# Softmax weights transposed by TensorE for every fourth query tile, in a fused attention and Fourier layer with a hand-written order on all engines

## The chip, the cores and the metric

One core of a Trainium2 chip runs the whole layer in one launch. The metric is the device time of one execution in microseconds. The numbers below come from three timed runs and from one further execution under the hardware profiler.

## What is computed

One trunk layer over 1024 latent tokens and 256 context tokens, model width 1024, all in float32. After a modulated layer norm and one input projection, one half of the mixing width is attention with 8 heads (96 query and key dimensions, 64 value dimensions, 1280 keys), the other half a 2-D Fourier mix. Both are gated, concatenated, projected and normalised. The part that matters here:

```python
def _softmax_attend(q, k, v):
    s = jnp.einsum("bqhd,bkhd->bhqk", q, k).astype(jnp.float32) * (1.0 / math.sqrt(QK_DIM))
    p = jax.nn.softmax(s, axis=-1).astype(v.dtype)
    return jnp.einsum("bhqk,bkhv->bqhv", p, v)
...
y = jnp.concatenate([attn * jax.nn.silu(g_mla), four * jax.nn.silu(g_f)], axis=-1)
return y @ w_out + b_out          # then x_new = layer_norm(alpha * x + gate * y) * g + b
```

## The kernel before

To keep float32 accuracy, operands are split into a high and a low part, and a product is three matmuls (high by high, high by low, low by high). The engines are called PE (TensorE, matmuls), DVE (VectorE), ACT (ScalarE), POOL (GpSimd) and SP (SyncE, which issues the DMAs).

The projections and the Fourier part run first (up to 277 us). Then a loop of 34 iterations handles 32 pairs of query tiles: a pair is one head and two tiles (j = 0, 1) of 128 queries. For a tile the steps are:

- `s_lat` (PE): scores against 1280 keys in three blocks a, b (512 columns each) and c (256), into the PSUM tile `SS[j]`;
- `max_lat` (DVE): one pass out of `SS[j]` that copies the negated scores to `E` in SBUF and keeps their minimum, a bias for the exponent; `bias` adds a constant to it;
- `exp` (ACT): the exponential in place in `E`, with the row sum;
- `hi` (ACT): the float16 high part `EH[:, 0]`; `lo` (POOL): the low part `EH[:, 1] = E - EH[:, 0]`, and then a transposing DMA, issued by SP, of both parts into `ET`, which has the keys on the partitions;
- `pv` (PE), two iterations later (`LAG = 2`), for both tiles of the pair: V by `ET` into a PSUM tile of the pool `tr`; `pv_top` (ACT) and `pv_out` (DVE) add its two halves into the attention output.

PSUM has 8 banks: `SS[0]` and `SS[1]` have three each (1280 of 1536 columns used), the pool `tr` has two buffers of one bank. `tr` also serves the fill work: keys (`build_kt`), V of the second half of the heads (`build_v`), queries (`build_qt`) and row factors (`finish_pair`), which are transposed or multiplied on PE and split by ACT and DVE. In SBUF, `E` and `EH` have three buffers of one tile, `ET` three of one pair.

Iteration n does the scores of pair n+1 (`nxt`), the late steps of pair n (marked with ') and the PV product of pair n-2. The string `SEQ` (`SEQ2` from n = 30) names the steps in order: S scores, m minimum, t bias, x exponential, h and l the two parts, P0 and P1 the halves of PV, Ra and Rv `pv_top` and `pv_out`, f one piece of fill work, `ga` and `gv` its postponed ACT and DVE parts, s one step of weight preparation, E output matmuls. The order is binding for PE alone (`MAN = 'P'`); on the other engines a planner with a cost model orders the instructions, and it may put later output matmuls into the loop.

Weight preparation (`prep(kt)`, kt = 0 to 7) makes the operands of the output projection: it loads 128 rows of `w_out`, multiplies them by a gate (DVE), splits them (POOL the high part, DVE the low part) and splits the mixed activations the same way. Row blocks 4 and 5 are prepared from iterations 24 and 27 in halves, 6, 7, 0 and 1 from iterations 30 to 33 in one piece, 2 and 3 behind the loop. The tail multiplies 8 token tiles by 8 row blocks (`out_mms`), adds, normalises (`finish`) and stores.

Of the kernel before, what the change touches and what calls it, by code (L numbers as in the profile page):

```python
# [21 lines left out]
P = 128  # L22
# [4 lines left out]
QK = 96  # L27
# [6 lines left out]
MAN = 'P'  # L34
SEQ = "ga S0 h1' l1' f P0 P1 ga Ra Rv m0 t0 s x0 s h0 l0 S1b S1c E0 E3 gv S1a m1 t1 f gv E2 x1 E1".split()
# [6 lines left out]
BIA = 'v'  # L42
SEQ2 = "S0c S0a h1' E1 l1' P0 S0b S1c P1 ga Ra Rv m0 t0 x0 h0 s s l0 ga S1b E0 E3 f gv S1a m1 t1 f gv E2 x1".split() or SEQ
# [19 lines left out]
def tile_hybrid_block(ctx: ExitStack, tc: tile.TileContext, a, out, dbg=None):  # L63
# [919 lines left out]
    pools["tr"] = at_ctx.enter_context(tc.tile_pool(name="ps_tr2", bufs=2, space=PSUM, reuse_waits="tile"))  # L983
    ps_s = at_ctx.enter_context(tc.tile_pool(name="ps_s", bufs=1, space=PSUM, reuse_waits="tile"))

    SS = [ps_s.tile([P, 1536], F32, tag=f"SS{j}", name=f"SS{j}") for j in range(2)]

    class Pair:
        def __init__(self, n):
            self.n, self.h, self.pr = n, n // 4, n % 4  # L990
            self.grp, self.e = self.h // 4, self.h % 2
            self.E, self.EH, self.ET = [None, None], [None, None], None
            self.mx = None
            self.po = None

# [132 lines left out]
    def prep(kt, alloc=None, n=1, parts=None):  # L1128

        raw = alloc(f"wor{kt}") if alloc else u4([P, D], F32, f"wor{kt}")  # L1130
        nc.sync.dma_start(out=raw, in_=a["w_out"][kt * P:(kt + 1) * P, :])
        part = parts or (lambda name: u4([P, D], F32R, name))
        wo[kt] = (part(f"woh{kt}"), part(f"wol{kt}"))
        mix[kt] = (part(f"mh{kt}"), part(f"ml{kt}"))
# [56 lines left out]
    early = {(0, 0): (0, 0), (0, 1): (0, 1), (1, 0): (1, 0), (1, 1): (1, 1)}  # L1191
    done = {}
# [6 lines left out]
    with tc.manual_schedule(engines={ET.PE}):  # L1199
        VA, VB = eval('(1,3)')  # L1200
        for i2 in range(VA):
            build_v(0, i2, False)
        p0.s_lat(0, 0)
        p0.s_lat(0, 1)
        p0.s_lat(0, 2)
        for i2 in range(VA, VB):
            build_v(0, i2, False)
        p0.max_lat(0)
        p0.bias(0)
        p0.exp(0)  # L1210
        if "h0'" not in SEQ:
            p0.hi(0)
        if "l0'" not in SEQ:
# [18 lines left out]
    with tc.manual_schedule(engines={{'P': ET.PE, 'V': ET.DVE, 'A': ET.Activation, 'G': ET.Pool, 'S': ET.SP}[c] for c in MAN}):  # L1232
        for n in range(NP + LAG):
# [4 lines left out]
            if n % 4 == 3 and n < NP - 1:  # L1238
                sum_rows(n // 4)
            fill = fills[n]  # L1240
            if n in FT['s']:
                steps += prep(4 + FT['s'].index(n), n=2)
            if n in LATE:
                steps += prep(ORDER[2 + LATE.index(n)])
            for op in (SEQ2 if n >= NSEQ2 else SEQ):
# [6 lines left out]
                if c in "SCmtxhlPR" and who is None:  # L1252
                    continue
# [4 lines left out]
                elif c == "m":  # L1258
                    who.max_lat(k)
                elif c == "t":  # L1260
# [59 lines left out]
    for kt in ORDER[2 + len(LATE):]:  # L1320
        for step in prep(kt, tl, parts=tw if kt in ORDER[-2:] else None):
# [50 lines left out]
    for t in range(3, 7):  # L1372
        ps = po_t(t)
        for i in range(8):
# [4 lines left out]
                  (tr("o70"), SS[1][:, 1024:1280], SS[0][:, 0:256])))  # L1379
# [75 lines left out]
```

## Time and profile before

| | us |
|---|---|
| three timed runs: median, lowest, highest | 634.28, 633.05, 636.16 |
| profiled execution: time, span of its instructions | 637.83, 636.1 |
| busy in the span: PE, DVE, ACT, POOL | 587.2, 391.9, 296.6, 302.1 |
| mean granted TensorE clock, share of full speed | 0.963 |

The span runs from the first to the last instruction of the profiled execution. An engine's busy time counts what it executes; waiting, branching and the issue of DMAs are not in it. Matmuls overlap each other, so that a matmul's own duration is longer than the distance to the next one, and PE's busy share is higher than its use. The granted clock is 1 at 2.4 GHz and 0.5 at 1.2 GHz. Times in the rows below count from the span's start.

### The profile page before, as it was taken

Reading aid. Unit: us, or ns where it says so; the run is one execution under the profiler, and the core shown is the slowest. Engines: PE = TensorE matmul, PEld = TensorE weight load, DVE = VectorE, ACT = ScalarE, POOL = GpSimd, SP = SyncE. Lnnn points to the kernel's source line nnn. Section 1 sums busy time; section 2 is a strip of 40 time slices with the busy share of each in tenths; the row PEclk is TensorE's granted clock in tenths of the full one; section 3 lists DMA queues with packets and bytes.
Section 4 is the critical chain, followed back from the end, with each engine's and each line's share of the span. In section 5 each row is a group of like instructions: output and inputs, shape, how many; then the busy total and the mean of one; then the engine's idle time right before and its main releaser. Section 6 shows DMA issues by size and latency. Waiting matters only on the chain.

```text
span 636.1 us, 9339 instructions
## 1 busy us (share of the span) xinstructions
PE 587.2 (92%) x3491; PEld 472.2 (74%) x3491; DVE 391.9 (62%) x742; ACT 296.6 (47%) x464; POOL 302.1 (47%) x233
## 2 busy tenths in 40 slices
PE   7999999999999998999999878999889877989994
PEld 6887777888899998988666656776656655668884
DVE  5538218611016588777566663677476887899567
ACT  2423521310125345488888895789678652100000
POOL 2123216011014186458768865787679876850000
PEclk8999999999999999999989987999889889899998
DMA  9999028000001122108999998799999998722302
GB/s 283 316 316 366 6 82 287 13 1 0 1 0 51 61 76 101 30 13 168 189 164 191 180 186 156 130 170 177 205 166 196 213 197 166 290 72 93 141 33 99
DMA packets 199701, 88.80 MB, mean 140 GB/s; under 512 B 168204, under 2 KB 189964, under 8 KB 199656
## 3 DMA queue, kind: packets, MB, share of 16 engines
q1 hardware_dynamic: 199656, 88.21, 59.7%
q8 instruction: 27, 0.44, 0.3%
q14 instruction: 18, 0.15, 0.1%
HBM read 41.39 MB, written 4.20 MB: 72 GB/s over the span
## 4 chain that ended last, share of the span: by engine, by line
PE 53%; DVE 14%; ACT 11%; DMA 8%; issue 6%; POOL 6%; SPq 1%; DVEq 0%; POOLq 0%; ACTq 0%
PE g L320 11%; PE fin L320 8%; PE SS L1154 7%; DMA ET<-EH 5%; ACT E L1029 4%; ACT EH L1038 4%; POOL EH L1046 4%; PE o L1154 3%; DVE E L1016 3%; DVE ml L83 2%; PE pv L1063 2%; PE tm L135 2%; PE tm L136 2%; PE tm L137 2%; PE SS L135 2%
## 5 line engine op out<-in xcount | busy, mean ns | idle before, releaser
L1046 POOL TENSOR_TENSOR EH<-E,EH 128x1280 f16<-128x1280 f32 x64 | 169.3, 2650 | 51.1 <-ACT EH L1038 41.8
L1016 DVE TENSOR_SCALAR_CACHE_REDUCE E<-SS 128x1280 f32<-128x1280 f32 x64 | 95.3, 1488 | 39.0 <-PE SS L137 27.0
L1029 ACT ACTIVATE E<-E,mx 128x1280 f32<-128x1280 f32 x64 | 86.8, 1357 | 23.9 <-DVE mx L1023 23.4
L1038 ACT ACTIVATE EH<-E 128x1280 f16<-128x1280 f32 x64 | 81.1, 1267 | 13.4 <-DMA ET<-EH 12.4
L1063 PE MATMUL pv<-ET,V 128*128 128x256 f16 x320 | 52.2, 300 | 18.8 <-DMA ET<-EH 6.5
L320 PE MATMUL fin<-h,wh 128*128 128x512 f32 x192 | 65.2, 407 | 0.0
L320 PE MATMUL g<-h,wh 128*128 128x512 f32 x192 | 60.2, 394 | 1.0 <-DVE upm L382 1.0
L135 PE MATMUL SS<-KTh,QT 96*128 96x512 f32 x128 | 56.3, 440 | 4.2 <-DVE E L1016 3.6
L1063 PEld LDWEIGHTS <-V 128*128 128x128 f16 x320 | 28.8, 105 | 35.9 <-issue 19.5
L136 PE MATMUL SS<-KTl,QT 96*128 96x512 f32 x128 | 51.8, 405 | 0.0
L137 PE MATMUL SS<-KTh,QT 96*128 96x512 f32 x128 | 51.8, 405 | 0.0
L320 PEld LDWEIGHTS fin<-h,wh 128*128 128x128 f32 x192 | 36.2, 189 | 10.3 <-issue 2.9
L320 PEld LDWEIGHTS g<-h,wh 128*128 128x128 f32 x192 | 36.0, 188 | 9.8 <-issue 1.4
L351 POOL TENSOR_SCALAR h<-xnT,mod 128x512 f32<-128x512 f32 x15 | 12.9, 859 | 63.2 <-ACT xnT L337 27.6
L111 ACT ACTIVATE rs_t<-mvf,eps 128x1 f32<-128x1 f32 x8 | 2.2, 293 | 81.4 <-DVE mvf L1342 77.3
L320 PE MATMUL g<-h,wl 128*128 128x512 f32 x96 | 37.8, 394 | 0.0
L320 PE MATMUL fin<-h,wl 128*128 128x512 f32 x96 | 37.1, 395 | 0.0
L1066 PE MATMUL pv<-ET,V 128*64 128x256 f16 x320 | 36.3, 304 | 0.0
L135 PEld LDWEIGHTS SS<-KTh,QT 96*128 96x128 f32 x128 | 24.9, 194 | 14.0 <-issue 6.6
L429 ACT ACTIVATE gt<-g,cols 128x512 f32<-128x512 f32 x12 | 8.1, 689 | 56.1 <-PE g L320 56.1
L1154 PE MATMUL SS<-woh,mh 128*128 128x512 f32 (+1 forms) x96 | 31.3, 384 | 2.4 <-POOL mh L82 1.3
L1352 POOL TENSOR_TENSOR xr<-xr,lng 128x256 f32<-128x256 f32 x2 | 1.4, 726 | 65.0 <-ACT xr L1351 65.0
(330 smaller groups left out, 1402.8 us busy)
## 6 DMA issues: line engine op xcount, KB each, us to landing
wada<-in_w_ada_dram SPq DMA_DIRECT2D x32, 256.0 KB, 6.0
x<-in_x_dram SPq DMA_DIRECT2D x8, 512.0 KB
wgate<-in_w_ada_dram SPq DMA_DIRECT2D x8, 512.0 KB, 6.6
wor<-in_w_out_dram SPq DMA_DIRECT2D x8, 512.0 KB, 4.1
xr<-in_x_dram SPq DMA_DIRECT2D x8, 512.0 KB, 9.9
out_dram<-xr SPq DMA_DIRECT2D x15, 256.0 KB, 2.1
wr<-in_w_in_dram SPq DMA_DIRECT2D x6, 512.0 KB, 5.5
wtr<-in_w_in_dram SPq DMA_DIRECT2D x4, 416.0 KB, 6.7
```

The source lines that it names most:

```text
L135: nc.tensor.matmul(ps, lhsT=sh, rhs=mh, start=(start and i == 0), stop=False)
L136: nc.tensor.matmul(ps, lhsT=sh, rhs=ml, start=False, stop=False)
L137: nc.tensor.matmul(ps, lhsT=sl, rhs=mh, start=False, stop=(i == n - 1))
L320: nc.tensor.matmul(ps, lhsT=(w.hi, w.lo, w.hi)[p][k][:, cs], rhs=h[:, p // 2], start=(k == 0 and p == 0), stop=(k == 7 and p == 2))
L351: nc.gpsimd.tensor_scalar(out=h, in0=xt, scalar1=sc, scalar2=sh, op0=ALU.mult, op1=ALU.add)
L1016: nc.vector.tensor_scalar(out=self.E[j], in0=SS[j][:, 0:1280], scalar1=0.0, scalar2=3e38, op0=ALU.add, op1=ALU.min, accum_out=self.mx[:, 2 ...
L1029: nc.scalar.activation(out=self.E[j], in_=self.E[j], func=AF.Exp, scale=-1.0, bias=self.mx[:, j:j + 1], accum_out=sums[self.h][:, qt:qt + 1])
L1038: nc.scalar.activation(out=o, in_=i, func=AF.Copy)
L1046: {"v": nc.vector, "p": nc.gpsimd}[eng].tensor_tensor(out=self.EH[j][:, 1, cs], in0=self.E[j][:, cs], in1=self.EH[j][:, 0, cs], op=ALU.sub ...
L1063: nc.tensor.matmul(po, lhsT=v.rearrange("p l c -> p (l c)"), rhs=e, start=(kt == 0), stop=False)
L1066: nc.tensor.matmul(po[64 * g:64 * g + 64], lhsT=v[:, 0], rhs=e, start=False, stop=(kt >= 8), tile_position=(0, 64 * g))
L1154: nc.tensor.matmul(ps[c], lhsT=st, rhs=w[:, c[0]:c[1]], start=(i == 0 and st is mh and w is wh), stop=(i == 7 and st is ml))
```

## The change

The scores of a pair go to three PSUM tiles: `SL[0]` and `SL[1]` (1024 columns, two banks each) for blocks a and b, and one shared bank `SC` for block c of both tiles. The freed bank gives `tr` a third buffer. The minimum is taken in two passes (`max_lat` over 1024, a new step c, `max_ctx`, over 256 columns), which the bias step joins.

For tile 1 of every pair with even n (16 of 64 tiles), `hi`, `lo` and the transposing DMA are replaced: PE transposes `E` in ten 128x128 blocks, in three groups of 4, 4 and 2 blocks, each in a `tr` buffer (T, `e_tr`); ACT copies the group to the high part in `ET` and DVE subtracts it for the low part (U, `e_out`). All five engines' orders are now the written one (`MAN = 'PVAGS'`), with new strings. Weight preparation starts at iterations 20, 23, 26 and 29 for blocks 4 to 7 and at 31 and 32 for 0 and 1, in halves, with the loads of `w_out` up to two iterations earlier; from iteration 30 on and in the tail ACT takes the high parts in place of POOL. Eight groups of output matmuls are named in the order. The diff, cut to its core:

```diff
-MAN = 'P'
-SEQ = "ga S0 h1' l1' f P0 P1 ga Ra Rv m0 t0 s x0 s h0 l0 S1b S1c E0 E3 gv S1a m1 t1 f gv E2 x1 E1".split()
+MAN = 'PVAGS'
+ON_PE = {(n, 1) for n in range(0, 32, 2)}
+KCUT = ((0, 1, 2, 3), (4, 5, 6, 7), (8, 9))
+SEQ = "S0b x1' gv S0a P0 s m0 P1 S0c l0' f c0 Ra h1' t0 Rv l1' gv T1a' S1b S1a U1a' T1b' m1 S1c T1c' ga x0 c1 ga t1 s U1b' h0 f U1c'".split()
-SEQ2 = "S0c S0a h1' E1 l1' P0 S0b S1c P1 ga Ra Rv m0 t0 x0 h0 s s l0 ga S1b E0 E3 f gv S1a m1 t1 f gv E2 x1".split() or SEQ
+SEQ2 = "S0b x1' gv S0a E P0 s s m0 P1 E E S0c l0' f c0 Ra h1' t0 Rv l1' gv T1a' S1b S1a U1a' T1b' m1 S1c T1c' ga x0 c1 ga t1 s s U1b' h0 f U1c' s s".split()
-LATE = eval('(30, 31, 32, 33)')
+INSIDE = (((4, 18, 20), (5, 22, 23), (6, 26, 26), (7, 28, 29)), ((0, 30, 31), (1, 31, 32)))
-FT = eval("{'k': [0, 0, 1], 'q': [1, 2], 'r': 4, 'p': [5, 5], 'v': [14, 14, 15, 15, 15], 'g': 22, 's': [24, 27]}")
+FT = eval("{'k': [0, 0, 1], 'q': [1, 2], 'r': 4, 'p': [5, 5], 'v': [11, 14, 15, 16, 17], 'g': 18}")
...
-    pools["tr"] = at_ctx.enter_context(tc.tile_pool(name="ps_tr2", bufs=2, space=PSUM, reuse_waits="tile"))
+    pools["tr"] = at_ctx.enter_context(tc.tile_pool(name="ps_tr2", bufs=3, space=PSUM, reuse_waits="tile"))
...
-    SS = [ps_s.tile([P, 1536], F32, tag=f"SS{j}", name=f"SS{j}") for j in range(2)]
+    SL = [ps_s.tile([P, 1024], F32, tag=f"SL{j}", name=f"SL{j}") for j in range(2)]
+    SC = ps_s.tile([P, 512], F32, tag="SC", name="SC")
...
+        def minimum(self, j, src, dst, c):
+            nc.vector.tensor_scalar(out=dst, in0=src, scalar1=0.0, scalar2=3e38, op0=ALU.add, op1=ALU.min,
+                                    accum_out=self.mx[:, c:c + 1])
...
+            self.minimum(j, SL[j], self.E[j][:, 0:1024], 2 + j)
+        def max_ctx(self, j):
+            self.minimum(j, SC[:, 256 * j:256 * j + 256], self.E[j][:, 1024:1280], 4 + j)
         def bias(self, j):
+            nc.vector.tensor_scalar(out=self.mx[:, j:j + 1], in0=self.mx[:, 2 + j:3 + j], scalar1=self.mx[:, 4 + j:5 + j],
+                                    scalar2=LIFT, op0=ALU.min, op1=ALU.add)
...
+        def e_tr(self, j, c):
+            self.weights_t()
+            kts = KCUT[c]
+            pt = self.pt[j, c] = tr("et")
+            for i, kt in enumerate(kts):
+                nc.tensor.transpose(pt[:, i * P:(i + 1) * P], self.E[j][:, kt * P:(kt + 1) * P], ident)
+        def e_out(self, j, c, what="av"):
+            k0, n = KCUT[c][0], len(KCUT[c])
+            pt = self.pt[j, c][:, 0:n * P].rearrange("p (k q) -> p k q", q=P)
+            hi, lo = self.ET[:, j, k0:k0 + n], self.ET[:, j, 10 + k0:10 + k0 + n]
+            if "a" in what:
+                nc.scalar.activation(out=hi, in_=pt, func=AF.Copy)
+            if "v" in what:
+                nc.vector.tensor_tensor(out=lo, in0=pt, in1=hi, op=ALU.subtract)
...
+    def load_wo(kt, alloc=None):
+        raws[kt] = alloc(f"wor{kt}") if alloc else u4([P, D], F32, f"wor{kt}")
+        nc.sync.dma_start(out=raws[kt], in_=a["w_out"][kt * P:(kt + 1) * P, :])
...
-        return {c: SS[c[0] // 512][:, 1024:1536] for c in HALVES}
+        return {HALVES[0]: SC, HALVES[1]: tr(f"o{t}")}
...
-    early = {(0, 0): (0, 0), (0, 1): (0, 1), (1, 0): (1, 0), (1, 1): (1, 1)}
+    early = [(t, i) for i in range(len(INSIDE[0])) for t in range(2)]
...
-            if n in FT['s']:
-                steps += prep(4 + FT['s'].index(n), n=2)
-            if n in LATE:
-                steps += prep(ORDER[2 + LATE.index(n)])
+            for kt, r, _ in INSIDE[0] + INSIDE[1]:
+                if n == r:
+                    load_wo(kt)
+            for kt, _, r in INSIDE[0] + INSIDE[1]:
+                if n == r:
+                    steps += prep(kt, how=split_ps if n >= NP - 2 else None)
...
-    for kt in ORDER[2 + len(LATE):]:
-        for step in prep(kt, tl, parts=tw if kt in ORDER[-2:] else None):
+    for kt in ORDER[sum(map(len, INSIDE)):]:
+        load_wo(kt, tl)
+        for step in prep(kt, 1, tw, split_ps):
```

## Rows read from the trace of the kernel before

**Rows 1.** Windows, by stage: busy us (instructions) of each engine, granted clock, DMA share, GB/s.

```profile
0.00:277.00 277.00, 269.07 (x1677) 232.51 (x1678) 136.74 (x311) 90.39 (x185) 81.51 (x118) 0.99 0.37 115
...
296.70:435.30 138.60, 126.51 (x786) 93.22 (x784) 85.10 (x162) 115.27 (x154) 103.46 (x50) 0.94 0.96 172
435.30:522.10 86.80, 74.88 (x447) 53.09 (x447) 62.52 (x102) 63.70 (x84) 68.52 (x38) 0.92 1.03 191
...
544.10:636.10 92.00, 80.52 (x369) 65.06 (x368) 75.37 (x127) 4.71 (x12) 20.42 (x12) 0.96 0.32 115
```

**Rows 2.** Timeline of PE: the start of the last pair's PV product.

```profile
540.70 0.71 PE L1063 MATMUL pv<-ET,V 128*128 128x256 f16 x5 [3.10 <-DMA ET<-EH]
```

**Rows 3.** Timeline of PE, one pair early in the loop: start us, us, what.

```profile
302.64 0.70 PE L1063 MATMUL pv<-ET,V 128*128 128x256 f16 x5
...
304.81 0.50 PE L135 MATMUL SS<-KTh,QT 96*128 96x512 f32 x1
...
305.38 0.39 PE L137 MATMUL SS<-KTh,QT 96*128 96x512 f32 x1
305.61 0.28 PE L135 MATMUL SS<-KTc,QT 96*128 96x256 f32 x1
```

**Rows 4.** Waits of PE in the loop, us in total, times, longest.

```profile
PE SS L135 <- DVE E L1016: 7.1, 3, 3.5
PE pv L1063 <- DMA ET<-EH: 6.5, 6, 3.1
PE pv L1063 <- DVE KTl L774: 5.9, 3, 3.2
PE pv L1063 <- DVE mx L1023: 3.9, 3, 1.8
```

**Rows 5.** Windows, same columns: the stretch in the loop that holds two long waits.

```profile
377.50:391.20 13.70, 11.12 (x47) 7.68 (x48) 7.25 (x15) 10.27 (x15) 7.86 (x3) 0.62 0.98 187
```

**Rows 6.** Lines by form in the loop: count | busy us, mean ns | idle before, releaser.

```profile
L1016 DVE TENSOR_SCALAR_CACHE_REDUCE E<-SS 128x1280 f32<-128x1280 f32 x62 | 92.3, 1488 | 38.2 <-PE SS L137 26.1 <-POOL EH L1046 9.4 <-PE pv L1066 1.6
...
L774 DVE TENSOR_TENSOR V<-v,V 128x512 f16<-128x512 f32 x7 | 4.7, 680 | 1.4 <-ACT V L772 1.3
...
L774 DVE TENSOR_TENSOR KTc<-kt,KTc 64x256 fp32r<-64x256 f32 x4 | 1.7, 421 | 0.4 <-ACT ckc_k L772 0.2 <-ACT KTc L772 0.2
...
L1029 ACT ACTIVATE E<-E,mx 128x1280 f32<-128x1280 f32 x63 | 85.5, 1357 | 23.7 <-DVE mx L1023 23.2
L1038 ACT ACTIVATE EH<-E 128x1280 f16<-128x1280 f32 x63 | 79.8, 1267 | 13.3 <-DMA ET<-EH 12.4
L1029 ACT ACTIVATION_READ_ACCUMULATOR E<-E,mx 128x1 f32 x63 | 11.7, 186 | 0.0
...
L772 ACT ACTIVATE V<-v 128x512 f16<-128x512 f32 x7 | 4.1, 591 | 2.7 <-PE v L137 2.5
L772 ACT ACTIVATE KTc<-kt 64x256 fp32r<-64x256 f32 x4 | 1.5, 379 | 0.1
...
L1046 POOL TENSOR_TENSOR EH<-E,EH 128x1280 f16<-128x1280 f32 x64 | 169.3, 2650 | 51.1 <-ACT EH L1038 41.8
```

**Rows 7.** Line 1050 on the SP queue: the transposing DMAs, issue ns minimum, median, maximum.

```profile
L1050 SPq DMA_TRANSPOSE ET<-EH x64: 2992/3105/5614, 284.9 to 534.9; - x64
```

**Rows 8.** Timeline of PE: the transposes of the row factors.

```profile
547.25 1.03 PE L1109 MATMUL r<-ident,rb 128*128 128x128 f32 x8
```

**Rows 9.** DVE in the loop: its wait for w_out, forms of weight preparation, one of them.

```profile
DVE wor L1139 <- DMA wor<-in_w_out_dram: 7.1, 3, 3.8
...
L83 DVE TENSOR_TENSOR ml<-gt,mh 128x512 fp32r<-128x512 f32 x4 | 8.1, 2040 | 0.0
...
L83 DVE TENSOR_TENSOR wol<-wor,woh 128x512 fp32r<-128x512 f32 x4 | 4.2, 1067 | 0.0
...
505.22 3.10 DVE L83 TENSOR_TENSOR ml<-gt,mh 128x512 fp32r<-128x512 f32 x1
```

**Rows 10.** Windows, line 1154 (output matmuls) alone: PE, PEld, granted clock, DMA share, GB/s.

```profile
522.10:544.10 22.00, 10.42 (x44) 7.75 (x43) 0.94 0.88 192
```

More of the change, by code (lines that the diff above doesn't have):

```diff
@@ L1126, in gate_rows, with prep @@
         gate.append(g)
[L1128 to L1134, printed above, removed]
+    raws = {}
+    def load_wo(kt, alloc=None):
+        raws[kt] = alloc(f"wor{kt}") if alloc else u4([P, D], F32, f"wor{kt}")
+        nc.sync.dma_start(out=raws[kt], in_=a["w_out"][kt * P:(kt + 1) * P, :])
+    def prep(kt, n=2, part=None, how=None):
+        part = part or (lambda name: u4([P, D], F32R, name))
+        how = how or split
         src = mixf[kt - 4] if kt >= 4 else gm[kt]
@@ L1138, in gated, with parts @@
         def gated(c):
-            nc.vector.tensor_tensor(out=raw[:, c], in0=raw[:, c], in1=gate[0][:, c], op=ALU.mult)
+            nc.vector.tensor_tensor(out=raws[kt][:, c], in0=raws[kt][:, c], in1=gate[0][:, c], op=ALU.mult)
+        def parts(to, name, c, x):
+            if kt not in to:
+                to[kt] = (part(f"{name}h{kt}"), part(f"{name}l{kt}"))
+            how(to[kt][0][:, c], to[kt][1][:, c], x[:, c])
         return ([lambda c=c: gated(c) for c in cs]
-                + [lambda c=c: split(wo[kt][0][:, c], wo[kt][1][:, c], raw[:, c]) for c in cs]
-                + [lambda c=c: split(mix[kt][0][:, c], mix[kt][1][:, c], src[:, c]) for c in cs])
+                + [lambda c=c: parts(wo, "wo", c, raws[kt]) for c in cs]
+                + [lambda c=c: parts(mix, "m", c, src) for c in cs])
     HALVES = ((0, 512), (512, 1024))
@@ L1207, in tile_hybrid_block @@
             build_v(0, i2, False)
[L1208 to L1211, printed above, removed]
+        if "m0'" not in SEQ:
+            p0.max_lat(0)
+        if "c0'" not in SEQ:
+            p0.max_ctx(0)
+        if "t0'" not in SEQ:
+            p0.bias(0)
+        if "x0'" not in SEQ:
+            p0.exp(0)
+        if "h0'" not in SEQ and not p0.on_pe(0):
             p0.hi(0)
-        if "l0'" not in SEQ:
+        if "l0'" not in SEQ and not p0.on_pe(0):
             p0.lo(0)
@@ L1219, in tile_hybrid_block @@
             build_v(0, i2, False)
-        p0.max_lat(1)
-        p0.bias(1)
-        p0.exp(1)
+        if "m1'" not in SEQ:
+            p0.max_lat(1)
+        if "c1'" not in SEQ:
+            p0.max_ctx(1)
+        if "t1'" not in SEQ:
+            p0.bias(1)
+        if "x1'" not in SEQ:
+            p0.exp(1)
         if "h1'" not in SEQ:
@@ L1251, in tile_hybrid_block @@
                     who = prv
-                if c in "SCmtxhlPR" and who is None:
+                if c in "SmctxhlPRTU" and who is None:
+                    continue
+                if c in "hlTU" and who.on_pe(k) != (c in "TU"):
                     continue
@@ L1286, in tile_hybrid_block @@
                 elif c == "E":
-                    if (n - NP + 1, k) in early:
-                        done[n] = done.get(n, -1) + 1
-                        t, i = early[n - NP + 1, done[n]]
+                    if n >= NP - 1 and early:
+                        t, i = early.pop(0)
+                        done.add((t, i))
                         if t not in pss:
@@ L1298, in tile_hybrid_block @@
                 late[ab].clear()
-            if n == NP - 1 or n == NP + LAG - 1:
+            if n % 4 == 3 and n < NP - 1:
+                sum_rows(n // 4)
+            if n == NP + LAG - 1:
                 while steps:
@@ L1367, in tile_hybrid_block @@
         for t in range(3):
-            if (t, i) not in early.values():
+            if (t, i) not in done:
                 out_mms(pss[t], t, i)
```

39 lines of the change are left out of this document (20 added, 19 removed).

## The prediction

> **What bounds the kernel now.** I read the stages first. Two fifths of the span are the loop of 32 pairs of query tiles, and the change is mostly there. In the first two loop stages TensorE (PE) is busy 91 and 86% of the time, ScalarE (ACT) 83 and 73%, GpSimd (POOL) 75 and 79%, VectorE (DVE) 61 and 72% [rows 1]. No engine is full; the reader is to see a pipeline in which four engines and the transposing DMA wait for each other.
>
> Next, what PE needs. The PV product begins its first pair at 296.7 and its last at 540.7 [rows 1, 2], so 31 pairs take 244 us, 7.87 each. Matmuls of 512 columns start 305.61 - 305.38 = 0.23 us apart, those of 256 at half of that, and a pair's PV takes 304.81 - 302.64 = 2.17 us [rows 3]. A pair's scores are 12 matmuls of 512 and 6 of 256 columns, 12 x 0.232 + 6 x 0.118 = 3.49; with PV 5.66 us. The rest of PE's work there is counted from the code: 3 key builds (18 of 512, 9 of 256), 30 V matmuls of 256, some 52 query and 24 row transposes at 0.107 (below), 48 output matmuls: 5.2 + 3.5 + 8.1 + 11.1 = 28. So 31 x 5.66 is 175, less some scores of the first pairs, issued before (8), plus 28: about 195 us. **Some 49 of 244 us are lost by PE.**
>
> Where? PE's waits: 7.1 us for DVE to empty a score tile, 6.5 for a transposing DMA, 5.9 and 3.9 at the start of PV behind DVE work that frees one of the two "tr" PSUM buffers: 23.4 [rows 4]. The granted clock is 0.94 and 0.92 in the two main loop stages, against 0.99 in the first 277 us [rows 1]: 6% of 244 us, up to 15 us of full-speed time. It fell where PE stood still: 0.62 in the 13.7 us that hold the two long waits before PV at 378 and 391 us [rows 5]. The other 10 us are gaps below these.
>
> **The change, part by part.**
>
> Transposes on TensorE. Every second pair (n even) sends tile 1 another way: 16 of 64 tiles. Each loses one f16 cast on ACT (1.27 us), one subtraction on POOL (2.65) and one transposing DMA (3.1 us of the SP queue) [rows 6, 7]. POOL's 169 us fall by 42, SP's 198 by 50. Neither is full, so this is worth only what waits on them. Each tile gains ten 128x128 transposes. The nearest row is the eight row-factor transposes, 1.03 us from the first start to the last end; less the last one's own length (0.28 at 256 columns) 0.75 / 7 = 0.107 apart [rows 3, 8]. So 1.07 us a tile; with a little for three entries, 1.15, times 16: **+18.4 us of PE work** (17.1 without; 27 if each burst costs 0.2 us of issue). Here is no cover: PE is the fullest engine.
>
> Their evacuation. ACT copies 512, 512 and 256 columns to f16: 2 x 0.59 + 0.38 = 1.56 against the 1.27 removed, +0.3 a tile. DVE subtracts: 2 x 0.68 + 0.42 = 1.78 a tile, +28 us in all [rows 6].
>
> The split minimum. DVE takes 1.49 us for 1280 columns. From 0.68 at 512 and 0.42 at 256 out of PSUM a column costs 1.04 ns and a start 0.155 us, so 1024 and 256 columns take 1.22 + 0.42, and with a second accumulator read, a tenth of a us at most, a tile costs 0.15 to 0.25 more: +10 to +16 us over 64, taken as 15 [rows 6]. DVE's idle time covers both (39% in the first stage); if that cover is gone they cost up to 43 us.
>
> Score tiles of 2, 2 and 1 banks leave a third "tr" buffer. It meets the 9.8 us in which PV waited behind DVE for one. But each PE-transposed tile now takes three such buffers in turn, whose last evacuation stands at the end of ACT's and DVE's order. I take 9 of 9.8 as gone and count the new waits below (bounds: 0 to 9.8 gone).
>
> Weight preparation. Each w_out load is issued two iterations or so ahead (only one for the last two) instead of in the iteration that uses it; DVE stood 7.1 us for them [rows 9], and the minima queued behind it kept score tiles from PE. Of the 7.1 us of score-tile waits I take 4.5 as gone (0 to 7.1). Of the DMA waits I take 4.5 of 6.5 (3 to 6.5): the last pair's tiles still go through the DMA. In the tail, two tiles' high parts move from POOL to ACT, which is idle there (4.7 of 92 us busy); PE is busy 80.5 of these 92 us, so I take nothing, within 3 us. The output products named early in the order are no gain: 44 of their matmuls run between 522 and 544 us already [rows 10]. Loads of "gate" and the V builds only change place.
>
> Order by hand. SP, DVE, ACT and POOL now run in the written order, so a late instruction holds back all behind it. On ACT the tile-1 exponential leads the iteration; behind it stand the PV copy, the PSUM copies and tile 0's exponential, which DMA and POOL wait for. ACT's need per two pairs: four exponentials of 1.54, three casts of 1.27, 1.56 of copies, two PV copies at the 0.38 of 256 columns, some 1.4 of evacuations: 13.8 us [rows 6]. PE's: 2 x 5.66 + 1.15 + 1.1 of builds = 13.6. Two engines nearly tie, so any wait of either is lost. New waits: nothing if the order fits, 1 us for each of the 16 tiles if the copy is late each time; the nearest existing ones, PV behind DVE, were 9.8 us for 32 pairs with two buffers. With three I take 3.
>
> **The sum.** Waits gone 9 + 4.5 + 4.5 = 18 of 23.4. The clock's 15 us go with them in proportion, 11. Against that 18.4 of transposes and 3 of new waits: -29 + 21.4 = -8 us. The profiled span 636.1 becomes 628 (execution 637.83 to 630); its execution lies 3.5 us above the median of 634.28, so against the median the same 8 us give 626.
>
> **A rule on the clock.** The first 277 us, which hold the 64 transposes of x between matmuls, keep a granted clock of 0.99 [rows 1]. The Trainium skill ("TensorE: Matmul & The Clock Gate", Part 4: PE-mode transpose) says that the full clock does not engage for transposes. By that rule the clock would fall at each of the new bursts (rival D); the trace of before, where transposes stand among matmuls, does not show it.
>
> **The rivals.**
>
> A. The order fits and nearly all waits go: 23.4 + 15 - 18.4 = -20, with part of the short gaps up to -26: 608 to 614, say 611. For it: loads, buffers and the DMA are each answered. Against: PE and ACT at 13.6 and 13.8 us would run without a slip.
>
> B. No change: ACT takes the place of the waits. Before, two pairs took 15.7 us; ACT needs 13.8. If its place in the chain costs 1.9 us per two pairs, the gain is gone: 634.
>
> C. Slower: DVE binds while weights are prepared (pairs 20 to 30, now 86.8 us or 7.9 a pair). Its need there: two minima 3.9, PV add 0.42, half of 1.78, small evacuations 0.7, and a third of one preparation, 2 x (0.68 + 1.07 + 2.04) / 3 = 2.5: 8.4 us a pair [rows 6, 9]. From 7.9 it decides. If, besides, DVE waits for POOL's high parts, queued behind 2.65 us subtractions, for 1 us in each of the four splits of a preparation, it is 9.7: 11 x 1.8 = +20, less some 8 gained in the first stage: 646; without those waits 632 to 638. I put it at 642. For it: one 512-column split took 3.10 us in the middle of POOL's subtractions, where 512 columns otherwise take 0.68 [rows 6, 9]. Against: a quarter less POOL work, and loads that arrive earlier. The Trainium skill ("SBUF — State Buffer", SBUF: two separate sides) calls this an exclusive lock: a DVE operation with two SBUF inputs waits out a GpSimd one. The trace agrees with the 3.10 us.
>
> D. The clock falls with each transposed tile. If only the bursts ran at 1.2 GHz, each would take 1.15 us more, 16 of them 18, and the 11 us of clock would not come back: 626 + 29 = 655, more if the matmuls behind them slow down too. The 0.99 of the first stage speaks against it [rows 1].
>
> **How the numbers follow.** The forecast has 0.45 (its own range 618 to 631, by the bounds of waits gone and entry cost), A 0.17, B 0.18, C 0.16, D 0.04. A change under 0.5% (3.2 us, about what can be told from none) counts as the same: faster 0.62, same 0.18, slower 0.20. The range leaves out the lower third of A, the upper half of C, and D, some 0.18 together: 609 to 642.
>
> **What would show it.** PV starts some 7.6 us apart on average over the loop instead of 7.87; 160 more transposes 0.11 us apart, three bursts each second pair; waits of PV for "tr" buffers and for the DMA mostly gone; granted clock 0.97 or more over the loop; DVE busier by 40 us. Wrong in the first place: PE waits at the transposes for the tile-1 exponential, or at PV for copies of the transposed tile; in the second: DVE without idle time from pair 20 on, with splits of 2 to 3 us.

## The result and the profile after

| | before | after |
|---|---|---|
| timed runs, us: median, lowest, highest | 634.08, 631.63, 637.49 | 639.66, 635.07, 643.84 |
| profiled execution: time, span | 637.83, 636.1 | 638.42, 636.6 |

Eighteen runs of each, in turn on the same chips, give a ratio of 1.0085, with an interval of 1.0066 to 1.0103: **slower by 0.85%, 5.6 us**. The two profiled executions differ by only 0.6 us, because the one of before lies 3.7 us above its median and the one of after 1.2 us below. A comparison of the two traces so shows where time moved, and about 5 us too little of the loss.

The windows view of after by stage, with the columns of [rows 1]; the loop is cut at PV starts:

```profile
0.00:277.00 277.00, 269.65 (x1692) 232.80 (x1693) 139.25 (x317) 91.20 (x187) 81.62 (x118) 1.00 0.37 115
277.00:294.70 17.70, 16.25 (x106) 14.35 (x104) 14.46 (x34) 15.11 (x24) 9.90 (x7) 1.00 0.33 63
294.70:424.40 129.70, 128.32 (x876) 97.31 (x875) 105.38 (x262) 113.99 (x171) 78.98 (x40) 1.00 0.77 143
424.40:528.80 104.40, 85.50 (x512) 61.36 (x511) 93.03 (x179) 67.90 (x101) 60.25 (x40) 0.90 0.67 134
528.80:544.10 15.30, 15.30 (x88) 11.14 (x88) 14.64 (x17) 7.88 (x13) 6.20 (x3) 1.00 0.65 149
544.10:636.60 92.50, 82.00 (x385) 66.77 (x384) 69.23 (x125) 8.83 (x16) 12.80 (x8) 0.95 0.31 114
```

The same cuts of before, at the first, nineteenth, thirtieth and last PV [rows 1, 2]: the first comes 2.0 us earlier (296.7 to 294.7); the next 18 pairs take 129.7 us instead of 138.6, at a granted clock of 1.00 instead of 0.94; then **eleven pairs take 104.4 instead of 86.8**, at 0.90 instead of 0.92; the last two take 15.3 instead of 18.6; and from the last PV to the end it is 92.5 instead of 95.4. Gains of 17.1 us stand against one loss of 17.6. In the losing stage DVE is busy 93.0 of 104.4 us (62.5 of 86.8 before) and every other engine is emptier than it.

PE's waits in that stage (us in total, times, longest) answer to [rows 4]. Waits for the DMA are gone, and PV no longer waits for a `tr` buffer, but now the transposes do (`et`, second line: `at` is the DVE sum that frees PV's buffer). All that is left waits for DVE:

```profile
PE SC L138 <- DVE E L1019: 9.1, 5, 4.6
PE et L1074 <- DVE at L1116: 6.4, 2, 4.4
PE pv L1097 <- DVE ET L1084: 3.0, 1, 3.0
```

DVE there, lines by form (count | busy us, mean ns | idle before), answers to [rows 6, 9]:

```profile
L1019 DVE TENSOR_SCALAR_CACHE_REDUCE E<-SL 128x1024 f32<-128x1024 f32 x22 | 26.7, 1214 | 0.1
L86 DVE TENSOR_TENSOR ml<-gt,mh 128x512 fp32r<-128x512 f32 x8 | 15.9, 1993 | 0.6 <-POOL mh L85 0.6
L1176 DVE TENSOR_TENSOR wor<-wor,gate 128x512 f32<-128x512 f32 x8 | 13.0, 1619 | 3.3 <-DMA wor<-in_w_out_dram 3.3
L86 DVE TENSOR_TENSOR wol<-wor,woh 128x512 fp32r<-128x512 f32 x8 | 10.1, 1262 | 1.5 <-POOL woh L85 1.5
L1019 DVE TENSOR_SCALAR_CACHE_REDUCE E<-SC 128x256 f32<-128x256 f32 x23 | 9.6, 417 | 2.9 <-PE SC L140 2.9
L1084 DVE TENSOR_TENSOR ET<-et,ET 128x512 f16<-128x512 f32 x11 | 7.5, 682 | 0.1
...
L1084 DVE TENSOR_TENSOR ET<-et,ET 128x256 f16<-128x256 f32 x5 | 2.1, 412 | 0.0
```

The 24 operations of weight preparation take 15.9 + 13.0 + 10.1 = 39.0 us. The same view of before, in its eleven pairs, has beside the 8.1 and 4.2 us of [rows 9]:

```profile
L1139 DVE TENSOR_TENSOR wor<-wor,gate 128x512 f32<-128x512 f32 x4 | 2.6, 688 | 5.8 <-DMA wor<-in_w_out_dram 5.8
L1139 DVE TENSOR_TENSOR wor<-wor,gate 128x1024 f32<-128x1024 f32 x1 | 2.0, 2046 | 0.0
...
L83 DVE TENSOR_TENSOR wol<-wor,woh 128x1024 fp32r<-128x1024 f32 x1 | 1.2, 1216 | 0.0
```

That is 18.1 us in all, for two blocks and a piece, where after prepares four. One place of the timeline of after shows the chain, DVE first, then POOL, then PE (start, length):

```profile
454.68 3.08 DVE L86 TENSOR_TENSOR ml<-gt,mh 128x512 fp32r<-128x512 f32 x1
457.68 1.01 DVE L1084 TENSOR_TENSOR ET<-et,ET 128x512 f16<-128x512 f32 x2
458.61 2.88 DVE L1176 TENSOR_TENSOR wor<-wor,gate 128x512 f32<-128x512 f32 x1
461.42 1.21 DVE L1019 TENSOR_SCALAR_CACHE_REDUCE E<-SL 128x1024 f32<-128x1024 f32 x1
...
462.56 0.41 DVE L1019 TENSOR_SCALAR_CACHE_REDUCE E<-SC 128x256 f32<-128x256 f32 x1
...
465.46 0.68 DVE L1176 TENSOR_TENSOR wor<-wor,gate 128x512 f32<-128x512 f32 x1
```

```profile
454.59 2.62 POOL L1055 TENSOR_TENSOR EH<-E,EH 128x1280 f16<-128x1280 f32 x1 [4.59 <-DVE E L1019]
458.35 2.60 POOL L1055 TENSOR_TENSOR EH<-E,EH 128x1280 f16<-128x1280 f32 x1 [1.13 <-ACT EH L1047]
```

```profile
458.04 0.40 PE L140 MATMUL SL<-KTh,QT 96*128 96x512 f32 x1
463.04 0.58 PE L138 MATMUL SC<-KTc,QT 96*128 96x256 f32 x1 [4.60 <-DVE E L1019]
463.42 0.42 PE L139 MATMUL SC<-KTc,QT 96*128 96x256 f32 x1
463.64 0.42 PE L140 MATMUL SC<-KTc,QT 96*128 96x256 f32 x1
463.85 0.63 PE L138 MATMUL SL<-KTh,QT 96*128 96x512 f32 x1
464.28 0.63 PE L139 MATMUL SL<-KTl,QT 96*128 96x512 f32 x1
```

Two DVE operations with both inputs in SBUF start inside POOL subtractions and end some 0.55 us behind them (457.76 behind 457.21, 461.49 behind 460.95); the same gate multiply takes 0.68 at 465.46, when POOL is idle. The minima queued behind these two start at 461.42 and 462.56; only then is the shared bank `SC` free, and PE has stood 4.60 us. PE goes on with 512-column matmuls 0.43 us apart instead of 0.23: the granted clock was 0.5 from 460.5 to 467.3. There are five such stretches in this stage, some 20 us in all, or 10 us of full-speed time.

The whole stage is like this: twelve of the 24 operations start 0.04 us or more after the start of a POOL subtraction and before its end, and each of them ends 0.54 to 0.56 us behind it. Six waits of PE in the stage are longer than 1 us, 18.0 us together, and the five stretches at 0.5 begin during or just behind five of these. Five of the six waits follow a DVE operation that waited POOL out. The sixth, 4.4 us at the transposes, has another start, DVE standing for a load of `w_out`:

```profile
487.64 1.14 DVE L1176 TENSOR_TENSOR wor<-wor,gate 128x512 f32<-128x512 f32 x1 [3.34 <-DMA wor<-in_w_out_dram]
490.90 0.87 PE L1074 MATMUL et<-ident,E 128*128 128x128 f32 x4 [4.43 <-DVE at L1116]
```

It is block 6, which `INSIDE` loads in the iteration that uses it: (6, 26, 26).

### The profile page after: what moved, and what is told of

Same layout as the page of the kernel before. It is cut to its first block, busy times and chain, and to the rows that moved or that the text cites. A ratio compares the mean times of both kernels' runs of the same rounds, so it can differ in the third digit from the quotient of the medians.

```text
span 636.6 us, 9858 instructions
## 1 busy us (share of the span) xinstructions
PE 597.0 (94%) x3651; PEld 483.7 (76%) x3651; DVE 436.0 (68%) x930; ACT 304.9 (48%) x508; POOL 249.7 (39%) x213
## 4 chain that ended last, share of the span: by engine, by line
PE 70%; DVE 12%; POOL 5%; DMA 4%; issue 4%; SPq 3%; ACT 2%; DVEq 0%; POOLq 0%
PE g L323 11%; PE fin L323 6%; PE SL L1196 6%; PE o L1196 5%; PE pv L1097 5%; PE pv L1100 4%; PE SL L138 3%; PE SL L139 3%; PE SL L140 3%; DVE E L1019 3%; PE tm L138 2%; PE tm L139 2%; PE tm L140 2%; DMA wada<-in_w_ada_dram 2%; PE SC L138 2%
## 5 line engine op out<-in xcount | busy, mean ns | idle before, releaser
L1055 POOL TENSOR_TENSOR EH<-E,EH 128x1280 f16<-128x1280 f32 x48 | 128.7, 2682 | 101.4 <-ACT EH L1047 55.8
L1038 ACT ACTIVATE E<-E,mx 128x1280 f32<-128x1280 f32 x64 | 86.8, 1357 | 23.1 <-DVE mx L1032 22.8
L1019 DVE TENSOR_SCALAR_CACHE_REDUCE E<-SL 128x1024 f32<-128x1024 f32 x64 | 77.8, 1216 | 4.3 <-PE SL L140 1.4
L1047 ACT ACTIVATE EH<-E 128x1280 f16<-128x1280 f32 x48 | 60.8, 1266 | 0.7
L138 PE MATMUL SL<-KTh,QT 96*128 96x512 f32 x128 | 54.9, 429 | 0.5 <-DVE tf L972 0.5
L139 PE MATMUL SL<-KTl,QT 96*128 96x512 f32 x128 | 51.8, 405 | 0.0
L140 PE MATMUL SL<-KTh,QT 96*128 96x512 f32 x128 | 51.6, 403 | 0.0
L1097 PE MATMUL pv<-ET,V 128*128 128x256 f16 x320 | 47.7, 281 | 3.6 <-DVE ET L1084 3.6
L1097 PEld LDWEIGHTS <-V 128*128 128x128 f16 x320 | 26.8, 100 | 22.8 <-issue 15.3
L1019 DVE TENSOR_SCALAR_CACHE_REDUCE E<-SC 128x256 f32<-128x256 f32 x64 | 26.8, 419 | 14.6 <-PE SC L140 14.4
L355 DVE TENSOR_TENSOR h<-h,h 128x512 fp32r<-128x512 f32 x15 | 13.6, 905 | 30.0 <-POOL h L354 22.7
L594 DVE TENSOR_TENSOR psb<-tm,btm 128x416 f32<-128x416 f32 x8 | 4.7, 590 | 42.3 <-PE tm L140 42.3
L1074 PE MATMUL et<-ident,E 128*128 128x128 f32 x160 | 26.6, 281 | 6.9 <-DVE at L1116 6.4
```

What stands on the lines that cost most here:

```text
L138: nc.tensor.matmul(ps, lhsT=sh, rhs=mh, start=(start and i == 0), stop=False)
L139: nc.tensor.matmul(ps, lhsT=sh, rhs=ml, start=False, stop=False)
L140: nc.tensor.matmul(ps, lhsT=sl, rhs=mh, start=False, stop=(i == n - 1))
L1019: nc.vector.tensor_scalar(out=dst, in0=src, scalar1=0.0, scalar2=3e38, op0=ALU.add, op1=ALU.min, accum_out=self.mx[:, c:c + 1])
L1038: nc.scalar.activation(out=self.E[j], in_=self.E[j], func=AF.Exp, scale=-1.0, bias=self.mx[:, j:j + 1], accum_out=sums[self.h][:, qt:qt + 1])
L1047: nc.scalar.activation(out=o, in_=i, func=AF.Copy)
```

## The experiments

All start from the kernel after unless another is named. Theories, by the letters that the expectations use: C, DVE binds in pairs 20 to 30, by weight preparation that waits out POOL's subtractions; O, the written order is what slips; T, the transposes cost PE more than they save. e1 and e5 leave out part of the computation.

| run | median us | ratio to before | 95% |
|---|---|---|---|
| e1_hi_only | 611.39 | 0.9631 | 0.9598 to 0.9663 |
| e2_prep_pool | 625.14 | 0.9849 | 0.9821 to 0.9878 |
| e3_no_pe | 636.93 | 1.0038 | 1.0018 to 1.0057 |
| e4_planner | 634.93 | 1.0016 | 0.9990 to 1.0042 |
| e5_memset | 611.66 | 0.9637 | 0.9603 to 0.9670 |
| e6_pool_no_pe | 640.14 | 1.0089 | 1.0061 to 1.0118 |
| e7_pool_planner | 643.40 | 1.0135 | 1.0101 to 1.0168 |
| e8_before_pool | 656.68 | 1.0335 | 1.0302 to 1.0367 |
| e9_act_hi | 619.15 | 0.9754 | 0.9728 to 0.9781 |
| e10_more_pe | 624.11 | 0.9831 | 0.9803 to 0.9859 |
| e11_late | 628.49 | 0.9892 | 0.9865 to 0.9919 |
| e12_earlier | 628.14 | 0.9905 | 0.9869 to 0.9940 |

**e1_hi_only**: blocks 4 to 7 without DVE.

```diff
-            nc.vector.tensor_tensor(out=raws[kt][:, c], in0=raws[kt][:, c], in1=gate[0][:, c], op=ALU.mult)
+            if kt < 4:
+                nc.vector.tensor_tensor(out=raws[kt][:, c], in0=raws[kt][:, c], in1=gate[0][:, c], op=ALU.mult)
...
+            if kt >= 4:
+                nc.gpsimd.tensor_scalar(out=to[kt][0][:, c], in0=x[:, c], scalar1=1.0, scalar2=0.0, op0=ALU.mult, op1=ALU.add)
+                return
```

> The changed kernel, leaving out part of the computation: for row blocks 4 to 7 of the weight preparation the gate multiplication and the low parts are left out (the high part stands for both), so that VectorE has no preparation work in the loop until block 0; GpSimd's high parts stay. Theory C (VectorE is the bound where weights are prepared, its two-input operations waiting out GpSimd's subtractions): the stretch of pairs 20 to 31, 104.4 us long in the changed kernel, falls by 17 to 24 us, and the time from 639.7 to 615 to 623. Theory T (the transposes and their evacuations cost more than they free): they are all still there, so the time stays at 632 to 640. Theory O (the written order itself is worse than the planner's): 632 to 640 as well.

Measured 611.39, 28 us below after and 4 below theory C's range. The windows view of its eleven pairs:

```profile
425.10:500.90 75.80, 75.40 (x513) 56.62 (x513) 60.13 (x153) 67.07 (x100) 56.12 (x39) 1.00 0.91 170
```

75.8 us instead of 104.4, at clock 1.00, with PE busy 75.4: all of the loss and more hangs on DVE's 24 operations in this stage, with the loads that they wait for. Whether on their own work or on POOL, this run doesn't tell; e5 does.

**e2_prep_pool**: the same work, all of it on POOL.

```diff
-        how = how or split
+        how = how or (lambda hi, lo, x: split(hi, lo, x, nc.gpsimd))
...
-            nc.vector.tensor_tensor(out=raws[kt][:, c], in0=raws[kt][:, c], in1=gate[0][:, c], op=ALU.mult)
+            (nc.gpsimd if kt >= 4 else nc.vector).tensor_tensor(out=raws[kt][:, c], in0=raws[kt][:, c], in1=gate[0][:, c], op=ALU.mult)
```

> The changed kernel with the whole preparation of row blocks 4 to 7 on GpSimd: gate multiplication, high and low parts. VectorE loses 39 us of busy time in the stretch of pairs 20 to 31, GpSimd gains some 25 to 30. Theory C: that stretch falls from 104.4 us to 85 to 95 and the time to 620 to 631, faster than the kernel before; not more, since GpSimd's subtractions for the scores now queue behind preparation. Theory T or O: 635 to 642.

Measured 625.14, 14.5 below after. The eleven pairs take 88.3 us (425.1 to 513.4). DVE is free, but POOL is full; the windows view of the stretch in which after loses:

```profile
424.40:528.80 104.40, 96.13 (x602) 69.78 (x601) 74.82 (x169) 74.91 (x112) 95.02 (x66) 0.97 0.74 146
```

POOL's 95.0 us is now what DVE's 93.0 was, and over the run DVE waits 20.7 us at the minima for `E` buffers that POOL still reads.

**e3_no_pe** and **e4_planner**: one part of the change undone in each.

```diff
-ON_PE = {(n, 1) for n in range(0, 32, 2)}
+ON_PE = set()
```

> The changed kernel with no tile transposed by TensorE; all 64 go through cast, subtraction and transposing DMA, in the same written order. Theory T: the time falls to 622 to 632 (18 us of transposes and 28 us of VectorE work are gone). Theory C: VectorE loses 9 us in the stretch of pairs 20 to 31 but GpSimd subtracts a quarter more and holds VectorE up longer, and before it the waits for the transposing DMA come back: 637 to 648. Theory O: 637 to 645, the order stays.

```diff
-MAN = 'PVAGS'
+MAN = 'P'
```

> The changed kernel with only TensorE's order written by hand, the planner ordering the other engines as before. Theory O: the planner finds better places, 620 to 632. Theory C: the planner moves VectorE's preparation into gaps, but the work and the waits behind GpSimd remain, and the first 20 pairs lose the 9 us that they won: 636 to 646. Theory T: 637 to 642.

Measured 636.93 and 634.93 against 639.66: without the transposes 2.7 us better, with the planner's order 4.7 better. Both times lie just outside all the ranges given. Neither alone explains 28 us. PE's waits in e3_no_pe:

```profile
PE SC L138 <- DVE E L1019: 23.9, 12, 4.9
PE pv L1097 <- DMA ET<-EH: 6.4, 6, 2.2
```

With sixteen more POOL subtractions the waits for `SC` behind DVE are 23.9 us instead of 9.1, and the waits for the DMA are back at 6.4, as in [rows 4]. So the transposes earn back in waits most of what they cost PE.

**e5_memset**: DVE keeps all its operations; POOL's subtraction is replaced by an operation that writes as much and reads nothing.

```diff
+                if self.n >= 20:
+                    nc.gpsimd.memset(self.EH[j][:, 1, cs], 0.0)
+                    continue
```

> The changed kernel, leaving out part of the computation: from pair 20 on GpSimd writes zeros as the low part of the exponentials instead of the subtraction, so that it reads nothing from SBUF for them; VectorE's preparation work is all there. Theory C with the waiting-out of GpSimd as its core: the 24 preparation operations of 512 columns fall from 1.3 to 2.0 us on average to about 0.7, the stretch of pairs 20 to 31 from 104.4 to 85 to 92 us, the time to 618 to 630. Theory C' (it is simply too much VectorE work, and the hand order leaves it no slack): the operations may shorten, but the time stays above 632. Part of any gain comes from a shorter GpSimd step; GpSimd was idle for 40% of that stretch.

Measured 611.66, as without DVE's operations, and 6 us below the range. Lines by form of DVE from 424 to 529 us, and the windows of pairs 20 to 30:

```profile
L1179 DVE TENSOR_TENSOR wor<-wor,gate 128x512 f32<-128x512 f32 x12 | 8.3, 709 | 2.4 <-DMA wor<-in_w_out_dram 2.4
...
L86 DVE TENSOR_TENSOR wol<-wor,woh 128x512 fp32r<-128x512 f32 x8 | 5.7, 715 | 0.5 <-POOL woh L85 0.5
L86 DVE TENSOR_TENSOR ml<-gt,mh 128x512 fp32r<-128x512 f32 x8 | 5.3, 678 | 0.3 <-POOL mh L85 0.3
```

```profile
424.80:503.80 79.00, 76.21 (x512) 56.32 (x511) 72.47 (x175) 66.68 (x99) 36.16 (x42) 1.00 0.87 172
```

1993, 1619 and 1262 ns have become 678, 709 and 715 while the same instructions stand in the same order. So 24 x 0.68 = 16.4 of the 39.0 us were work and 22.6 were spent waiting POOL out, and the stage falls from 104.4 to 79.0. POOL is also less busy in this run (its memset takes 1.16 us instead of 2.7), so tiles reach the DMA earlier; but no PE wait for POOL or the DMA stood in after's stage that this could have removed. In this stage PE still waits 1.7 us at the transposes behind the load of block 6.

**e6_pool_no_pe** and **e7_pool_planner**: e3 and e4 again, on top of e2's edit, where DVE is free.

> Preparation of blocks 4 to 7 on GpSimd and, besides, no tile transposed by TensorE. If the transposes pay once VectorE is free (what they were costed for), this is slower than with them: 630 to 640 against 625.1, for GpSimd then has 16 more subtractions beside the preparation. If the transposes cost more than they free in any case (theory T): 618 to 625.

> Preparation of blocks 4 to 7 on GpSimd, with the planner ordering all engines but TensorE. If the written order is good in itself and only the preparation spoilt it: slower than 625.1, 628 to 635. If the written order costs some 5 us whatever the preparation does, as the run with the planner alone suggests (634.9 against 639.7): 618 to 623.

Measured 640.14 and 643.40 against e2's 625.14. With DVE free the transposes are worth 15.0 us and the written order 18.3; with DVE full they were worth -2.7 and -4.7. e7 lies 8 us above the highest range. In e6 PE's waits say where the transposes pay (e2 has 3.4 us for the DMA and 2.9 for `SC`), in e7 what the planner does to the shared bank:

```profile
PE pv L1097 <- DMA ET<-EH: 18.5, 13, 3.1
PE SC L138 <- DVE E L1019: 10.0, 11, 2.7
```

```profile
PE SC L138 <- DVE E L1019: 20.9, 3, 12.2
```

**e8_before_pool**: e2's edit in the kernel before.

```diff
-            nc.vector.tensor_tensor(out=raw[:, c], in0=raw[:, c], in1=gate[0][:, c], op=ALU.mult)
+            (nc.gpsimd if kt >= 4 else nc.vector).tensor_tensor(out=raw[:, c], in0=raw[:, c], in1=gate[0][:, c], op=ALU.mult)
...
-                + [lambda c=c: split(wo[kt][0][:, c], wo[kt][1][:, c], raw[:, c]) for c in cs]
+                + [lambda c=c: split(wo[kt][0][:, c], wo[kt][1][:, c], raw[:, c], nc.gpsimd if kt >= 4 else None) for c in cs]
```

(and the same for `mix`)

> The kernel before the change with the preparation of blocks 4 to 7 on GpSimd. There GpSimd was the engine that the transposing DMA waited for, and only two blocks are prepared before the scores end. Theory C as told, with the change's relief of GpSimd as the condition for moving work there: 632 to 642, no gain. If the move to GpSimd helps any version: 624 to 630, and the gain of 625.1 owes little to the change.

Measured 656.68, 22 above before and 15 above the range. Moving preparation to POOL is no gain of its own: before, POOL carries all 64 subtractions. e2 and e6 say the same: they differ in the 16 tiles alone, and take 625 and 640 us. But e8 also has the planner's order, which costs 18 us in e7; how much of the 22 us is POOL's work and how much the order isn't separated.

**e9_act_hi**, **e10_more_pe**, **e11_late**: ways to free DVE. In e9 ACT makes the high parts, POOL multiplies by the gate (as in e2) and makes the low parts, and block 6 is loaded an iteration earlier. e10 adds five PE-transposed tiles to e9. e11 leaves the work on DVE and starts it later; its blocks 0 and 1 are prepared from iterations 32 and 33, not from 31 and 32 as its expectation says.

```diff
+    def split_ag(hi, lo, x):
+        nc.scalar.activation(out=hi, in_=x, func=AF.Copy)
+        nc.gpsimd.tensor_tensor(out=lo, in0=x, in1=value(hi), op=ALU.subtract)
...
-        how = how or split
+        how = how or split_ag
...
-INSIDE = (((4, 18, 20), (5, 22, 23), (6, 26, 26), (7, 28, 29)), ((0, 30, 31), (1, 31, 32)))
+INSIDE = (((4, 18, 20), (5, 22, 23), (6, 25, 26), (7, 28, 29)), ((0, 30, 31), (1, 31, 32)))
```

> As the kernel with the whole preparation of blocks 4 to 7 on GpSimd (625.1), but the high parts on ScalarE and the load of block 6 one iteration earlier. In that kernel GpSimd worked without a gap from 453 to 526 us but for 4.1 us that it stood for the load of block 6, and VectorE waited 17.8 us for it. GpSimd sheds 16 x 0.62 = 10 us and the wait. Theory C (what is late is GpSimd's queue): 613 to 621. If ScalarE, which leads the chain, has no room for 16 more copies of 0.59 us: 623 to 630.

```diff
-ON_PE = {(n, 1) for n in range(0, 32, 2)}
+ON_PE = {(n, 1) for n in range(32) if n % 2 == 0 or 20 <= n < 31}
```

> The same, and from pair 20 on TensorE transposes tile 1 of every pair, not of every second one: 5 tiles more, so 13 us less on GpSimd, 6 us more on TensorE, 9 more on VectorE. If GpSimd still bounds the stretch: 610 to 618. If TensorE bounds it by then (7.1 us a pair): 617 to 625.

```diff
-INSIDE = (((4, 18, 20), (5, 22, 23), (6, 26, 26), (7, 28, 29)), ((0, 30, 31), (1, 31, 32)))
+INSIDE = (((4, 22, 24), (5, 26, 27), (6, 29, 30), (7, 30, 31)), ((0, 31, 32), (1, 32, 33)))
```

> The changed kernel (VectorE prepares) with the preparation later, as in the kernel before: blocks 4, 5, 6, 7, 0, 1 from iterations 24, 27, 30, 31, 31 and 32 instead of 20, 23, 26, 29, 31 and 32; loads one or two iterations ahead. Theory C: half of the 24 operations leave the stretch in which the scores need VectorE: that stretch 8 to 12 us shorter, 2 to 8 of it given back at the end, where the output products wait for blocks 6 and 7: 630 to 638. If it is only the amount of VectorE work, wherever it stands: 638 to 642.

Measured 619.15, 624.11 and 628.49. **e9 beats both kernels**, by 2.5% and 3.2%. Its eleven pairs take 81.8 us. Its windows view from 424.4 to 520 us, and POOL's lines by form there:

```profile
424.40:520.00 95.60, 90.90 (x592) 66.60 (x591) 73.05 (x168) 82.19 (x128) 84.86 (x50) 1.00 0.83 162
```

```profile
L1055 POOL TENSOR_TENSOR EH<-E,EH 128x1280 f16<-128x1280 f32 x19 | 50.8, 2686 | 1.2 <-ACT EH L1047 1.2
L1170 POOL TENSOR_TENSOR ml<-gt,mh 128x512 fp32r<-128x512 f32 x8 | 10.7, 1337 | 0.3 <-ACT mh L1169 0.3
L1170 POOL TENSOR_TENSOR wol<-wor,woh 128x512 fp32r<-128x512 f32 x8 | 10.4, 1303 | 6.3 <-issue 5.8 <-POOL wor L1180 0.5
L1180 POOL TENSOR_TENSOR wor<-wor,gate 128x512 f32<-128x512 f32 x8 | 10.3, 1289 | 2.0 <-DMA wor<-in_w_out_dram 2.0
```

The preparation costs POOL 31.4 us, less than the 39.0 it cost DVE, although one such operation takes POOL 1.3 us and DVE 0.68. Four engines now stand at 73 to 91 of 95.6 us. In e10 the added transposes lose 5 us, as expected if PE bounds: from 475.9 to 511.5 us it is busy without a gap, at 6.9 us or more a pair. e11 gains 11.2 us over after with DVE's work at other places, or nearly so: blocks 6 and 7 also get their high parts from ACT, as from iteration 30 on, and block 6 is loaded an iteration ahead, so that DVE stands 0.3 us for `w_out` in the loop. Of the three e11 says most of the change itself: the placement of preparation, loads included, was part of the loss.

**e12_earlier**: e9 with preparation one iteration earlier or so, to empty the last pairs.

```diff
-INSIDE = (((4, 18, 20), (5, 22, 23), (6, 26, 26), (7, 28, 29)), ((0, 30, 31), (1, 31, 32)))
+INSIDE = (((4, 18, 19), (5, 21, 22), (6, 24, 25), (7, 27, 28)), ((0, 30, 31), (1, 31, 32)))
```

> The fastest kernel so far (preparation of blocks 4 to 7 on GpSimd with the high parts on ScalarE, 619.15 us) with this preparation one iteration earlier, from iterations 19, 22, 25 and 28. There the last four pairs took 8.2, 9.2 and 9.7 us between their PV products, where block 7 on GpSimd meets the last subtractions and the preparation of blocks 0 and 1 on VectorE. If that meeting costs what it seems to: 615 to 618. If the gate row or the loads are then late, or the end is set by something else: 619 to 623.

Measured 628.14, 9 us slower than e9 and 5 above the range. In the traced execution, the fastest of eight (623.52), POOL, in the written order, stood for the gate row, whose load had not landed:

```profile
POOL wor L1180 <- DMA gate<-gsum: 7.0, 1, 7.0
```

That pair took 13.5 us from PV to PV instead of 9.3, and the last three still took 9.6, 9.2 and 8.8. The long pair is about what the traced execution lost to e9's median (4.4 us); the 4.6 us by which e12's own median lies above it no trace shows. Why the last pairs of e9 take 8 to 10 us stays open.

## Why the prediction was wrong

626 us and "faster" were forecast; 639.66 and slower by 0.85% came. The range to 642 holds the time, by rival C, which had 0.16.

- **Where it was right.** The price of the transposes: less PE's waits (27.9 us before, 20.3 after, all that the view lists) and the clock's loss (15 and 10), the loop from first PV to last grew by 18 us, and 18.4 were forecast; four transposes mostly took 0.35 or 0.36 us to the next instruction (0.43 worked out). The waits for the DMA are gone in the whole loop, and PV waits for no `tr` buffer. The first stage gave 2.0 + 8.9 us, with its clock at 1.00. Durations: 1.21 and 0.42 us for the two minima (1.22 and 0.42 worked out), 0.68 and 0.41 for the subtractions. DVE's busy time rose by 44 us (391.9 to 436.0), forecast 28 + 15 = 43; the two parts came (28.4 and 14.5), but the closeness of the total is luck, since the rows of the bias steps (4) and of preparation (8) grew too and overlap hides about as much.
- **The clock rule (rival D) fell.** 160 transposes stand in bursts of 4, 4 and 2 among matmuls, and the eighteen pairs that hold more than half of them ran at 1.00. The Trainium skill ("TensorE: Matmul & The Clock Gate", Part 4: PE-mode transpose) has the full clock not engage for transposes. Where they stand among matmuls, this trace does not agree.
- **The step that failed is the price of the moved preparation.** "Weight preparation" took 4.5 us of score-tile waits as gone, and put no cost on four blocks now standing in these eleven pairs where two and a piece stood. Twelve halves at 0.68 and two whole ones at 1.22 are 10.6 us, so 16.4 - 10.6 = 6 us of work and 22.6 - (18.1 - 10.6) = 15 us of waiting for POOL came with it. The time from the last PV to the end fell by 2.9 us only. The same paragraph has each load of `w_out` two iterations ahead, or one; block 6's is issued in the iteration that uses it, and PE's wait of 4.4 us stands behind that.
- **With it fell "DVE's idle time covers both"**, said of the evacuations and the split minimum, with its evidence "39% in the first stage". The cover was read in a stage that has it and used in one that hasn't. In pairs 20 to 30 DVE was already busy 62.5 of 86.8 us before [rows 1]. There the change adds, in the lines by form, 9.6 us of evacuations, some 5 of minima (39.8 with the accumulator reads against 34.4 for 22 tiles), 2 for a bias step with two pointer operands, and 39.0 - 18.1 = 20.9 of preparation: 38 us of rows (some overlap; busy time rose by 30.5). e5 shows which of these used the cover up: it has all of them but the waiting, and its stage is 79.0 us, shorter than before's 86.8.
- **"New waits ... I take 3"** became 18.5 in this stage, 9.1 of them for the bank `SC` that both tiles share: a minimum late in DVE's written order stops the next pair's scores. Less these 18.5 us and the clock's 10, the 104.4 us are 76, what the stage takes in e1 (75.8). Over the whole loop, of the 23.4 us of waits in [rows 4] and 3 new ones, some 8 were to be left; 19.1 are: 9.1 for score tiles (7.1 before), 6.4 for `tr` buffers (9.8), 3.6 at PV for DVE's part of a transposed tile, none for the DMA (6.5). The clock's loss fell from 15 to 10 us, where 11 were to come back: the loop ran at 0.96, and 0.97 or more was the sign. So PV starts 8.05 us apart, not 7.6.
- **Rival C had the place, and in its evidence the mechanism.** It put DVE's need at 8.4 us a pair, up to 9.7; DVE was busy 93.0 / 11 = 8.5 and the pair took 9.5. Its step from 8.4 to 9.7, 1 us of waiting for POOL's high part in each of 16 splits, was not it: DVE stood 2.1 us for them. The time went into the operations themselves, like the one of 3.10 us that C quotes; that its 9.7 is so near 9.5 is in part luck. The Trainium skill ("SBUF — State Buffer", SBUF: two separate sides) makes the lock one against a GpSimd operation that reads SBUF. e5 agrees, with 0.68 to 0.72 us beside a memset and 1.26 to 1.99 beside subtractions. What C argued against itself, a quarter less POOL work, did not help: POOL was busy 60 of 104 us, and a single subtraction in the wrong place holds DVE for up to 2.4 us.

So the change's parts are good for the first eighteen pairs and pay in full once DVE is free (e6, e7), and its own placement of the preparation takes the gain back. Not settled: how much of e11's gain is the place, how much ACT's high parts and how much the load of block 6, and, since stage times come from one execution each, which stage holds the 5 us by which the medians differ more than the two traces.

## What to carry to other kernels

Look for cover in the stage where the work will stand, not in the average: an engine at 61% in one stage was the bound in the next. Price a VectorE operation with two SBUF inputs by what GpSimd is doing beside it (here 0.68 us alone, 1.3 to 2.0 on average beside subtractions, 3.1 at worst); such work may be cheaper on GpSimd itself, at 1.3 us each, where GpSimd has room (e2 and e9, but not e6 and e8). When parts of a change each test as useless, test them again with the bound removed: the same two parts went from -3 and -5 us to +15 and +18.

## What the runs showed of the hardware

- A GpSimd memset of 128x1280 in f16 (1.16 us) beside the same VectorE instructions left them at 0.68 to 0.72 us; beside the subtraction that reads and writes SBUF one took 3.08, and the twelve that started inside one ended 0.54 to 0.56 us behind it.
- The bias step, a VectorE operation on 128x1, took 0.214 us with two operands read from SBUF and 0.147 us with one value and constants, 64 times in either kernel.
- With bursts of fp32 transposes between matmuls the granted clock stayed at 1.00 for 129.7 us.
